# Retention in chunks of 128 tokens with carried states, in place of all keys by all queries, in a two-layer diffusion backbone

## The chip, the cores and the metric

The kernel runs on one core of one Trainium2 chip. The metric is the device time of one execution in microseconds. Three timed runs of the kernel before gave a median of 2387.9 us (2387.57 to 2388.31).

## What is computed

The network has two layers. In each, a modulated norm is followed by one wide input projection, whose columns feed three mixers (a convolution, an attention and a retention), whose outputs are gated, summed and projected; then comes a gated feed-forward part. The latent stream has 512 tokens, the context stream 256; the second layer computes queries for latents only. The change touches the retention. Its reference, for 8 heads of 64 features, runs over chunks of 128 tokens with a state of 64x64 per head, once forward and once backward; the scans of the latents start from the states that the scans of the context end with:

```python
def step(state, inp):
    qc, kc, vc = inp
    inner = jnp.einsum('bihd,bjhd->bhij', qc, kc) * decay_in
    o = (jnp.einsum('bhij,bjhe->bihe', inner, vc)
         + jnp.einsum('bihd,bhde->bihe', qc * q_dec[:, :, None], state))
    state = state * chunk_dec[:, None, None] + jnp.einsum('bjhd,bjhe->bhde', kc * k_dec[:, :, None], vc)
    return state, o

o_cf, s_f = retention_scan(q_c, k_c, v_c, log_gamma[0], s0)
o_cb, s_b = retention_scan(flip(q_c), flip(k_c), flip(v_c), log_gamma[1], s0)
o_lf, _ = retention_scan(q, k, v, log_gamma[0], s_f)
o_lb, _ = retention_scan(flip(q), flip(k), flip(v), log_gamma[1], s_b)
```

## The kernel before

Activations lie feature by token: a tile of 128 features by 768 tokens, latents in columns 0 to 511 and context in 512 to 767. A dense product takes every float32 operand as two float32r parts (`hh` and `hl` for activations, `whi` and `wlo` for weights) and sums three products of parts in PSUM (`chunk`, `dense`, L242 to L254); its tiles in PSUM are called `pd` and have four banks, all other products (`ps`) have the other four. Weights stream through SBUF once; ScalarE and VectorE split each tile of 1024 columns into its parts (`prepare`, L99).

The mixers are generators that run beside the dense products: after every product `tick` gives each of them credit, and each `yield` of a generator spends some (L222, L148). That sets the order in which the program is written; the scheduler of the framework then orders each engine's own list, and an engine works through its list in order. `layer_mixers` (L1273) goes through the units of `ORDER`. A unit P (`ret_inputs`, L1154) makes three dense products for a pair of heads: keys, queries and gate. The retention of the pair, `ret_gen` (L709), is run by `mixers` (L1288) once the attention is done, beside the units P of the next pairs and the gates T; there are four pairs in each layer.

The retention takes all keys by all queries. For each pair of heads, `evac_split` (L578) splits keys and queries into float32r parts, and `stack` (L1145) lays the parts of a head above each other by transfers on GpSimd's queue, so that one product with 128 rows makes two of the three products of parts and one with 64 rows the third. For each of the six key tiles there are two score tiles of 128 keys by 512 queries (and 256 context queries in the first layer), which VectorE multiplies by the decays (tile `rsc`, L750). `decay` (L689) makes the decays of one head for all distances, five exponentials on ScalarE and four operations on VectorE. Then `pv` multiplies the scores by the values in plain float32, 64 output rows for each head side by side, and sums over the key tiles in PSUM.

After that (L763 on, not changed) come the squares, the product with a block matrix (`ro`), the reciprocal root and the gate.

Of the kernel before, what the change touches and what calls it, by code (L numbers as in the profile page):

```python
"""Hybrid conv / GQA / retention DiT backbone on one core.

Activations are feature-major: a [128, T] tile per 128 features, with the latent tokens in
columns 0..511 and the context tokens in columns 512..767. Dense products run on the tensor
engine in float32r: every float32 operand is split exactly into two float32r parts and three
products of parts are accumulated. Weights stream through SBUF once, in the order of use.
"""
# [8 lines left out]
F32 = mybir.dt.float32  # L16
# [6 lines left out]
P = 128  # L23
# [10 lines left out]
SUB = 1024                      # columns of a weight tile  # L34
NSUB = 140                      # weight tiles of a layer
START = ((0, 256, 2), (256, 256, 0), (512, 256, 4), (768, 256, 0))  # columns of the first modulation, weight tiles after
ND = 4                          # PSUM banks of the dense products
RAWB, RAWA = 2, 2               # tiles of raw weights, of raw w_ada
WB = 4                          # split weight tiles
NSLOT = 47                      # activation tiles  # L40
# per layer: order of the units of the input projection (K keys and values, Q queries, R retention values,
# A attention and retention begin, G inputs of the convolution, C it begins, P retention heads, T gates)
ORDER = ('K Q0 R0 Q1 A R1 G0 C G1 G2 G3 P0 P1 P2 P3 T T T T',
         'K Q0 Q1 R0 A G0 C R1 G1 G2 G3 P0 P1 P2 P3 T T T T T T')
ATT_LEAD, RET_LEAD = (3, 2), (1, 1)   # head pairs by which the mixers may lag behind the projection
# [1548 lines left out]
```

## Time and profile before

| what | value |
|---|---|
| timed runs | 2387.9 us median of 3 (2387.57 to 2388.31) |
| span of the profiled execution, first to last instruction | 2385.8 us (its own time is not listed apart) |
| TensorE (PE) busy | 2347.9 us, 98% of the span |
| VectorE (DVE) busy | 1566.2 us, 66% |
| ScalarE (ACT) busy | 896.0 us, 38% |
| chain that ended last | PE 95%, DVE 3%, issue 1%, DMA 1% |
| mean DMA rate | 98 GB/s |

Busy time is the time in which an engine had at least one instruction in work; matmuls overlap at their ends, so the busy times of single groups add up to more than the engine's. What a group costs the engine is read from the distance between starts, or from what is left of a stretch when all else in it is taken off.

### The profile page before, as it was taken

The page shows a single profiled execution, that of the slowest core. Times are in us where ns is not written, and L with a number is a line of the kernel's source. Part 1 is how long each engine was busy: PE and PEld are TensorE (multiplying, and loading weights), DVE is VectorE, ACT ScalarE, POOL GpSimd, SP SyncE. Part 2 cuts the span into 40 slices and gives each one's busy share as a digit, 9 for nine tenths or more (in the row PEclk, how much of TensorE's full clock was granted, in tenths as well). Part 3 has the DMA queues.
Part 4 walks back from the last instruction along what each step waited for, and adds up shares of the span by engine and source line. Part 5 has one row for each costly group of instructions (what it writes and reads, how often), then busy time and mean ns, then how long its engine had stood idle before and what let it go on. Part 6 is the DMA issues. An engine that isn't in the chain of part 4 may idle for free.

```text
span 2385.8 us, 33890 instructions
## 1 busy us (share of the span) xinstructions
PE 2347.9 (98%) x13426; PEld 1941.3 (81%) x13426; DVE 1566.2 (66%) x3174; ACT 896.0 (38%) x1505; POOL 62.6 (3%) x122
## 2 busy tenths in 40 slices
PE   6999999999999999999999999999999999999998
PEld 5988876678888888888888889887558889888887
DVE  6887858688874476645763359878688546544445
ACT  3465644422232342213122234565443433423233
POOL 0000010000000000000000000001100000000000
PEclk9999999999999999999999999999999999999999
DMA  7221122213343123323661121113223322332322
GB/s 287 96 65 60 63 80 69 71 62 115 107 142 105 54 73 118 118 97 101 210 210 62 62 98 54 55 61 102 70 67 112 131 98 80 106 97 97 97 97 71
DMA packets 69119, 234.13 MB, mean 98 GB/s; under 512 B 8640, under 2 KB 10960, under 8 KB 68960
## 3 DMA queue, kind: packets, MB, share of 16 engines
q1 hardware_dynamic: 59616, 203.64, 25.8%
q0 software_dynamic: 9344, 28.32, 4.1%
q8 instruction: 106, 1.74, 0.3%
q14 instruction: 53, 0.43, 0.1%
HBM read 213.57 MB, written 6.82 MB: 92 GB/s over the span
## 4 chain that ended last, share of the span: by engine, by line
PE 95%; DVE 3%; issue 1%; DMA 1%; ACT 0%; SPq 0%; DVEq 0%; ACTq 0%
PE pd L197 81%; PE ps L197 12%; PE ps L1090 2%; DVE ht L543 0%; DVE wlo L108 0%; PE ps L1003 0%; DVE hl L555 0%; DMA x<-xt 0%; DVE qq L1038 0%; DMA raw<-wstream 0%; ACT whi L107 0%; DVE sq L508 0%; DVE mod L418 0%; DVE rstdt L491 0%; DVE rstd L492 0%
## 5 line engine op out<-in xcount | busy, mean ns | idle before, releaser
L197 PE MATMUL pd<-hl,whi 128*128 128x512 f32 (+1 forms) x2176 | 658.6, 354 | 1.9 <-DVE hl L555 1.7
L197 PE MATMUL pd<-hh,wlo 128*128 128x512 f32 (+1 forms) x2176 | 659.9, 355 | 0.0
L197 PE MATMUL pd<-hh,whi 128*128 128x512 f32 (+1 forms) x2176 | 656.9, 354 | 1.4 <-DVE fy L1387 0.9
L107 ACT ACTIVATE whi<-raw 128x1024 fp32r<-128x1024 f32 x280 | 296.7, 1061 | 930.9 <-PE pd L197 840.6
L108 DVE TENSOR_TENSOR wlo<-raw,whi 128x1024 fp32r<-128x1024 f32 x280 | 341.6, 1221 | 261.8 <-ACT whi L107 258.7
L197 PEld LDWEIGHTS pd<-hh,whi 128*128 128x128 f32 x2176 | 361.9, 188 | 69.5 <-issue 8.3
L197 PEld LDWEIGHTS pd<-hl,whi 128*128 128x128 f32 x2176 | 360.3, 188 | 68.9 <-issue 8.3
L197 PEld LDWEIGHTS pd<-hh,wlo 128*128 128x128 f32 x2176 | 360.8, 188 | 64.6 <-issue 9.4
L608 DVE SCALAR_TENSOR_TENSOR cacc<-u,vec,cacc 128x497 f32<-128x497 f32 (+9 forms) x360 | 221.4, 648 | 1.9
L197 PE MATMUL pd<-hidh,wlo 128*128 128x512 f32 (+1 forms) x558 | 169.1, 348 | 0.0
L197 PE MATMUL pd<-hidh,whi 128*128 128x512 f32 (+1 forms) x558 | 167.9, 346 | 0.0
L197 PE MATMUL pd<-hidl,whi 128*128 128x512 f32 (+1 forms) x558 | 167.3, 345 | 0.0
L1073 ACT ACTIVATE prob<-ps,amx,qrs 128x256 f32<-128x256 f32 (+1 forms) x144 | 93.7, 656 | 90.8 <-DVE amx L1068 77.5
L197 PE MATMUL pd<-whi,hl 128*128 128x256 f32 x416 | 120.1, 289 | 3.9 <-DVE hl L555 3.9
L197 PE MATMUL pd<-whi,hh 128*128 128x256 f32 x416 | 120.5, 292 | 2.8 <-ACT hh L552 2.8
L197 PE MATMUL pd<-wlo,hh 128*128 128x256 f32 x416 | 119.3, 287 | 0.0
L1430 DVE SCALAR_TENSOR_TENSOR x<-pd,mod,x 128x512 f32<-128x512 f32 (+1 forms) x102 | 62.1, 632 | 81.0 <-PE pd L197 80.7
L466 DVE SCALAR_TENSOR_TENSOR rowa<-rowa,crow 128x768 f32<-128x768 f32 (+1 forms) x144 | 94.2, 686 | 26.2 <-DMA rowa<-wadt 26.2
L197 PEld LDWEIGHTS pd<-hidh,whi 128*128 128x128 f32 x558 | 94.9, 189 | 14.9 <-issue 0.2
L1395 DVE TENSOR_TENSOR fy<-fy,pd 128x512 f32<-128x512 f32 x66 | 37.5, 596 | 104.2 <-PE pd L197 101.4
L197 PEld LDWEIGHTS pd<-hidl,whi 128*128 128x128 f32 x558 | 93.7, 188 | 14.1 <-issue 0.2
L197 PEld LDWEIGHTS pd<-hidh,wlo 128*128 128x128 f32 x558 | 94.3, 189 | 13.0
(236 smaller groups left out, 3251.4 us busy)
## 6 DMA issues: line engine op xcount, KB each, us to landing
raw<-wstream SPq DMA_DIRECT2D x280, 512.0 KB, 3.5
rowa<-wadt SPq DMA_DIRECT2D x72, 512.0 KB, 4.1
adar<-wada SPq DMA_DIRECT2D x16, 384.0 KB, 7.6
stk<-rkh POOLq DMA_DIRECT2D x32, 192.0 KB, 4.9
rawa<-wada SPq DMA_DIRECT2D x8, 512.0 KB, 3.6
x<-xt SPq DMA_DIRECT2D x8, 384.0 KB, 7.6
x<-xt POOLq DMA_DIRECT2D x8, 384.0 KB, 4.4
adar<-wada SPq DMA_DIRECT2D x8, 256.0 KB, 7.5
```

The costliest lines, as they stand in the source:

```text
L107: nc.scalar.activation(hi, r, AF.Copy)
L108: nc.vector.tensor_tensor(lo, r, hi.bitcast(F32), op=ALU.subtract)
L197: return self.nc.tensor.matmul(out, w, x, start=start, stop=stop)
L466: nc.vector.scalar_tensor_tensor(out, raw[:, a:b], 1.0, t[:, o:o + b - a], op0=ALU.mult, op1=ALU.mult, accum_out=acc[:, c, j, h:h + 1])
L608: nc.vector.scalar_tensor_tensor(acc[:, a:b], u[:, a + d:b + d], w(k), acc[:, a:b], op0=ALU.mult, op1=ALU.add)
L1073: nc.scalar.activation(pr[:, o - k0:o - k0 + c], pt[:, :c], AF.Exp, scale=rs, bias=mx[:, 2:3], accum_out=sm[:, j:j + 1])
L1090: nc.tensor.transpose(pt[:, b * P:b * P + P], pr[:, o + b * P:o + b * P + P], self.ident)
L1395: nc.vector.tensor_tensor(y[:, o:o + n], y[:, o:o + n], pt, op=ALU.mult)
L1430: nc.vector.scalar_tensor_tensor(xs[m][:, s], pt, g2[:, m, j:j + 1], xs[m][:, s], op0=ALU.mult, op1=ALU.add)
```

## The change

It replaces the retention by the chunkwise form of the reference, for the two heads of a pair side by side in the 128 features.

- Keys and queries stay plain float32 (`plain`): no split, no `stack`, no transfers for them.
- TensorE transposes the six key tiles to token-major; VectorE multiplies them by the decays to the end and to the start of a chunk (`kf`, `kb`).
- Scores are made only between tokens of the same chunk: for each chunk and head a float32 product with 64 rows, 128 by 128, the two heads on the two halves of the rows. VectorE multiplies them by a decay of 128x128 that is the same for all chunks.
- Ten products of 128x128 make the contributions of the chunks to the forward and backward states of both heads (the blocks between different heads are masked to zero with `blk`); VectorE scales them and carries the states from chunk to chunk (`stf`, `stb`, L796 after the change).
- The outputs of a pair are summed in PSUM: the scores by the values, 64 rows for each head, and the states by the decayed queries (`qf`, `qb`), with all 128 rows.
- `decay(p)` makes six exponentials of 128 columns for a pair. `ret_tables` makes small tables once in a layer.
- `pe_order` keeps the products of a group in order on TensorE; with arguments, the first product of the group waits for those instructions, so that the group doesn't begin before all of its operands are there.

The diff, cut to the new code (the code that it replaces is printed above; comments are left out):

```diff
 @@ in place of evac_split(), decay(h), stack() and the body of ret_gen()
+    def ret_tables(self):
+        nc = self.nc
+        self.kdec, self.lgx, self.gx = self.sm(16, "kdec"), self.sm(8, "lgx"), self.sm(8, "gx")
+        ij = self.ij
+        for d in range(2):
+            nc.scalar.activation(self.kdec[:, 8 * d:8 * d + 8], self.lg[:, 8 * d:8 * d + 8], AF.Exp,
+                                 scale=ij[:, 4 * P + d:4 * P + d + 1])
+        l4 = self.lg.rearrange("q (c t) -> q c t", t=2)
+        for t in range(2):
+            r = slice(64 * t, 64 * t + 64)
+            nc.vector.tensor_copy(self.lgx[r].rearrange("q (c o) -> q c o", o=1), l4[r, :, t:t + 1])
+        nc.scalar.activation(self.gx, self.lgx, AF.Exp, scale=float(P))
+    def decay(self, p):
+        nc = self.nc
+        w = self.S("dec")
+        ij = self.ij
+        ex = lambda o, i, sc: nc.scalar.activation(w[:, o * P:o * P + P], ij[:, i * P:i * P + P], AF.Exp, scale=sc)
+        for t in range(2):
+            h = 2 * p + t
+            ex(t, 0, self.lg[:, h:h + 1])
+            ex(2 + t, 1, self.lg[:, 8 + h:9 + h])
+        ex(4, 2, self.lgx[:, p:p + 1])
+        ex(5, 3, self.lgx[:, 4 + p:5 + p])
+        f, b = (w[:, o:o + 2 * P].rearrange("p (t i) -> p t i", t=2) for o in (0, 2 * P))
+        for x, m in ((f, self.mf), (b, self.mb)):
+            nc.vector.tensor_tensor(x, x, m.rearrange("p (o i) -> p o i", o=1).to_broadcast([P, 2, P]), op=ALU.mult)
+        nc.vector.tensor_tensor(w[:, 0:2 * P], w[:, 0:2 * P], w[:, 2 * P:4 * P], op=ALU.add)
+        return w
+    @contextmanager
+    def pe_order(self, *after):
+        traced = self.nc.cur_bb.bb.instructions
+        n = len(traced)
+        yield
+        info = lambda c: mybir.DependencyInfo(c, mybir.DependencyReason.DATA)
+        last = None
+        for i in traced[n:]:
+            if i.engine != mybir.EngineType.PE:
+                continue
+            if last:
+                self.tc.add_manual_dep(i, last, info(mybir.DependencyClass.NoSync), reason="order")
+            else:
+                for a in after:
+                    self.tc.add_manual_dep(i, a.ins.name, info(mybir.DependencyClass.Sync), reason="together")
+            last = i.name
+    def ret_gen(self, p, rk, rq, sg, ctxq):
+        nc = self.nc
+        nq = 6 if ctxq else 4
+        w = self.decay(p)
+        yield 2.5
+        bc = lambda t, n: t.rearrange("p (o i) -> p o i", o=1).to_broadcast([P, n, P])
+        v3 = lambda t, n: t.rearrange("p (c i) -> p c i", c=n)
+        tile = lambda t: slice(t * P, t * P + P)
+        heads = lambda hh: slice(64 * (2 * p + hh), 64 * (2 * p + hh) + 64)
+        kt = [self.ps(), self.ps()]
+        with self.pe_order():
+            for t in range(6):
+                nc.tensor.transpose(kt[t // 4][:, tile(t % 4)], rk[:, tile(t)], self.ident)
+        kf, kb = self.S("kf"), self.S("kb")
+        def keys(d, dst, o, src, a, n):
+            dec = self.kdec[:, 8 * d + 2 * p:8 * d + 2 * p + 2].rearrange("p (o h e) -> p o h e", o=1, e=1)
+            return nc.vector.tensor_tensor(
+                dst[:, o * P:(o + n) * P].rearrange("p (c h d) -> p c h d", c=n, h=2),
+                src[:, a * P:(a + n) * P].rearrange("p (c h d) -> p c h d", c=n, h=2),
+                dec.to_broadcast([P, n, 2, 64]), op=ALU.mult)
+        keys(0, kf, 0, kt[1], 0, 2)
+        keys(1, kb, 0, kt[1], 0, 2)
+        keys(0, kf, 2, kt[0], 0, 3)
+        last_k = keys(1, kb, 2, kt[0], 1, 3)
+        yield 1.0
+        scs = [self.S("rsc") for _ in range(2)]
+        lasts = []
+        for a, n in ((0, 4), (4, 2))[:1 + ctxq]:
+            pts = [self.ps() for _ in range(2)]
+            with self.pe_order():
+                for t in range(n):
+                    for hh, pt in enumerate(pts):
+                        r = slice(64 * hh, 64 * hh + 64)
+                        self.mm(pt[:, tile(t)], rk[r, tile(a + t)], rq[r, tile(a + t)], t == 0, t == n - 1)
+            for hh, (sc, pt) in enumerate(zip(scs, pts)):
+                lasts.append(nc.vector.scalar_tensor_tensor(
+                    v3(sc[:, a * P:(a + n) * P], n), v3(pt[:, :n * P], n), 0.125, bc(w[:, tile(hh)], n),
+                    op0=ALU.mult, op1=ALU.mult))
+            yield 0.25 * n
+        F, B = self.S("stf"), self.S("stb")
+        order = ([(kf, 0, 4), (kf, 1, 5), (kf, 2, 0), (kf, 3, 1)],
+                 [(kb, 1, 5), (kb, 0, 4), (kb, 4, 3), (kb, 3, 2)],
+                 [(kf, 4, 2), (kb, 2, 1)])
+        sts = []
+        with self.pe_order(last_k):
+            for part in order:
+                st = self.ps()
+                sts.append(st)
+                for j, (k, i, t) in enumerate(part):
+                    self.mm(st[:, tile(j)], k[:, tile(i)], self.rv[t][:, 2 * p * 64:2 * p * 64 + P], j == 0,
+                            j == len(part) - 1)
+        scale = lambda o, i, n: nc.vector.scalar_tensor_tensor(
+            v3(o, n), v3(i, n), 8.0, bc(self.blk, n), op0=ALU.mult, op1=ALU.mult)
+        scale(F[:, :4 * P], sts[0], 4)
+        scale(B[:, :4 * P], sts[1], 4)
+        scale(F[:, 4 * P:5 * P], sts[2][:, :P], 1)
+        scale(B[:, 4 * P:5 * P], sts[2][:, P:2 * P], 1)
+        for j in range(1, 5):
+            for d, x in enumerate((F, B)):
+                nc.vector.scalar_tensor_tensor(x[:, tile(j)], x[:, tile(j - 1)], self.gx[:, 4 * d + p:4 * d + p + 1],
+                                               x[:, tile(j)], op0=ALU.mult, op1=ALU.add)
+        qf, qb = self.S("qf"), self.S("qb")
+        for x, n, o in ((qf, nq, 4), (qb, nq - ctxq, 5)):
+            lasts.append(nc.vector.tensor_tensor(v3(x[:, :n * P], n), v3(rq[:, :n * P], n), bc(w[:, tile(o)], n),
+                                                 op=ALU.mult))
+        yield 2.6
+        yield 1.0
+        po = self.ps()
+        pc = self.ps() if ctxq else None
+        with self.pe_order(*lasts):
+            for t in range(nq):
+                out, j = (po, t) if t < 4 else (pc, t - 4)
+                for hh, sc in enumerate(scs):
+                    self.mm(out[64 * hh:64 * hh + 64, tile(j)], self.rv[t][:, heads(hh)], sc[:, tile(t)], j == 0, False)
+            for t in range(4):
+                self.mm(po[:, tile(t)], F[:, tile(1 + t)], qf[:, tile(t)], False, False)
+                self.mm(po[:, tile(t)], B[:, tile(4 - t)], qb[:, tile(t)], False, t == 3)
+            if ctxq:
+                self.mm(pc[:, tile(1)], F[:, tile(0)], qf[:, tile(5)], False, False)
+                self.mm(pc[:, tile(0)], B[:, tile(0)], qb[:, tile(4)], False, True)
+        yield 2.9 + 0.8 * ctxq
+        segs = ALL if ctxq else LAT
...
+    def plain(self, pts, m, name):
+        t = self.S(name)
+        for pt, o, c in pts:
+            self.nc.scalar.activation(t[:, o:o + c], pt, AF.Identity, bias=self.bias_col(m))
+        return t
+    def ret_inputs(self, p, segs, T):
+        rk = self.plain(self.win(18 + p, ALL), 18 + p, "rk")
+        self.tick(self.cost)
+        rq = self.plain(self.win(14 + p, segs), 14 + p, "rq")
+        self.tick(self.cost)
+        pg = self.win(26 + p, segs)
...
 @@ in mixers()
-            self.ii, self.jj = self.S("ii"), self.S("jj")
-            nc.gpsimd.dma_start(self.ii, io["ij"][0])
-            nc.gpsimd.dma_start(self.jj, io["ij"][1])
+            self.ij = self.S("ij")
+            nc.gpsimd.dma_start(self.ij[:, :4 * P + 2], io["ij"])
+            self.ret_tables()
...
 @@ in _shape_constants()
-    ij = np.stack([np.maximum(t[None] - p[:, None], 0), np.maximum(640 + p[:, None] - t[None], 0)]).astype(np.float32)
+    i, j = p[None] + 0 * p[:, None], p[:, None] + 0 * p[None]
+    ij = np.concatenate([np.maximum(i - j, 0), np.maximum(j - i, 0), i + 1, P - i, P - 1 - p[:, None], p[:, None]],
+                        1).astype(np.float32)
```

On TensorE, for the first pair of heads of the first layer, before: `stk` are stacked parts of keys and queries, `rqh` and `rkl` the parts of the third product, `rsc` the decayed scores, `rv` the values.

```order
L197 MATMUL ps_4049<-rsc_4063,rv_826 64x512
L197 MATMUL ps_4049<-rsc_4064,rv_826 64x512
L197 MATMUL ps_4089<-stk_3647,stk_3454 128x512
L197 MATMUL ps_4090<-stk_3650,stk_3457 128x512
L197 MATMUL ps_4089<-rqh_3641,rkl_3449 128x512
L197 MATMUL ps_4090<-rqh_3641,rkl_3449 128x512
L197 MATMUL ps_4049<-rsc_4075,rv_826 64x512
L197 MATMUL ps_4049<-rsc_4076,rv_826 64x512
```

Two key tiles stand here; a pair has six of them, with scores of 512 queries each, and dense products lie between some of them.

On TensorE, for the second pair of the first layer, now, behind the transposes, four pairs of latent scores and thirteen dense products among them: `rq`, `rk` are queries and keys of both heads, `kf`, `kb` the decayed keys.

```order
L197 MATMUL pd_4435<-hh_410,whi_4123 128x512
L197 MATMUL ps_4367<-rq_4177,rk_4011 128x128
L197 MATMUL ps_4366<-rq_4177,rk_4011 128x128
L197 MATMUL ps_4367<-rq_4177,rk_4011 128x128
L197 MATMUL ps_4376<-rv_827,kf_4346 128x128 x2
L197 MATMUL ps_4376<-rv_826,kf_4346 128x128 x2
L197 MATMUL ps_4381<-rv_827,kb_4347 128x128 x3
L197 MATMUL ps_4381<-rv_826,kb_4347 128x128
L197 MATMUL ps_4386<-rv_826,kf_4346 128x128
L197 MATMUL ps_4386<-rv_826,kb_4347 128x128
```

The context scores and the states' contributions follow each other; then 27 dense products stand before the scores by the values.

On VectorE, for the first pair of the first layer, before: `deca`, `decb` are the decays of a head, `cacc` the convolution.

```order
L750 SCALAR_TENSOR_TENSOR rsc_4087<-ps_4089,deca_3957 128x512
L750 SCALAR_TENSOR_TENSOR rsc_4088<-ps_4090,deca_4037 128x512
L750 SCALAR_TENSOR_TENSOR rsc_4099<-ps_4101,decb_3958 128x512
L750 SCALAR_TENSOR_TENSOR rsc_4100<-ps_4102,decb_4038 128x512
L750 SCALAR_TENSOR_TENSOR rsc_4099<-ps_4109,deca_3957 128x256
L750 SCALAR_TENSOR_TENSOR rsc_4100<-ps_4110,deca_4037 128x256
L599 TENSOR_SCALAR cacc_4120<-u_2589,vec_86 128x768
L608 SCALAR_TENSOR_TENSOR cacc_4120<-u_2589,vec_86,cacc_4120 128x497
```

And now, for the second pair: `kdec`, `dec`, `gx` are decays, `kf` and `kb` the keys (the last of four), `stf` and `stb` the states.

```order
L752 TENSOR_TENSOR kb_4347<-ps_4338,kdec_3937 128x384
L771 SCALAR_TENSOR_TENSOR rsc_4352<-ps_4354,dec_4328 128x512
L771 SCALAR_TENSOR_TENSOR rsc_4353<-ps_4355,dec_4328 128x512
L771 SCALAR_TENSOR_TENSOR rsc_4352<-ps_4366,dec_4328 128x256
L771 SCALAR_TENSOR_TENSOR rsc_4353<-ps_4367,dec_4328 128x256
L788 SCALAR_TENSOR_TENSOR stf_4374<-ps_4376,cst 128x512
L788 SCALAR_TENSOR_TENSOR stb_4375<-ps_4381,cst 128x512
L788 SCALAR_TENSOR_TENSOR stf_4374<-ps_4386,cst 128x128
L788 SCALAR_TENSOR_TENSOR stb_4375<-ps_4386,cst 128x128
L796 SCALAR_TENSOR_TENSOR stf_4374<-stf_4374,gx_3939 128x128
L796 SCALAR_TENSOR_TENSOR stb_4375<-stb_4375,gx_3939 128x128
```

The last two operations stand three times more, then `qf` and `qb` (768 and 640 columns) close the chain; in this pair no operation of the convolution stands inside it, and 26 to 31 of them stand between one chain and the next.

## Rows read from the trace of the kernel before

**Rows 1.** the profile's page, parts 1 and 4: busy time; the chain that ended last
```profile
PE 2347.9 (98%) x13426; PEld 1941.3 (81%) x13426; DVE 1566.2 (66%) x3174; ACT 896.0 (38%) x1505; POOL 62.6 (3%) x122
...
PE 95%; DVE 3%; issue 1%; DMA 1%; ACT 0%; SPq 0%; DVEq 0%; ACTq 0%
```

**Rows 2.** two stretches, PE: length, busy (instructions), granted clock, DMA share, GB/s
```profile
330.00:512.00 182.00, 182.00 (x846) 1.00 0.24 66
1653.50:1792.00 138.50, 138.50 (x552) 1.00 0.28 74
```

**Rows 3.** PE's groups by form from 330 to 512: busy, mean ns, idle before
```profile
L197 PE MATMUL pd<-hh,whi 128*128 128x512 f32 x95 | 38.6, 406 | 0.0
...
L197 PE MATMUL ps<-rsc,rv 128*64 128x512 f32 x96 | 36.2, 615 | 0.0
...
L197 PE MATMUL pd<-hh,whi 128*128 128x256 f32 x96 | 27.3, 284 | 0.0
```

**Rows 4.** PE's groups by form from 1653.5 to 1792
```profile
L197 PE MATMUL pd<-hl,whi 128*128 128x512 f32 x100 | 41.3, 413 | 0.0
...
L197 PE MATMUL pd<-hh,whi 128*128 128x256 f32 x17 | 4.9, 291 | 0.0
```

**Rows 5.** timeline of PE, dense products alone: start us, us, form, count
```profile
899.71 0.53 PE L197 MATMUL pd<-hh,wlo 128*128 128x512 f32 x2
...
904.66 0.51 PE L197 MATMUL pd<-hl,whi 128*128 128x512 f32 x2
...
1659.18 0.39 PE L197 MATMUL pd<-hh,whi 128*128 128x512 f32 x1
...
1664.39 0.39 PE L197 MATMUL pd<-hh,wlo 128*128 128x512 f32 x1
```

**Rows 6.** timeline of PE, one key tile without dense products
```profile
345.08 0.73 PE L197 MATMUL ps<-stk,stk 128*128 128x512 f32 x2
345.74 0.50 PE L197 MATMUL ps<-rqh,rkl 64*128 64x512 f32 x2
346.17 1.08 PE L197 MATMUL ps<-rsc,rv 128*64 128x512 f32 x4
347.18 0.73 PE L197 MATMUL ps<-stk,stk 128*128 128x512 f32 x2
```

**Rows 7.** timeline of PE, transposes and plain float32 products of 128 to 512 columns
```profile
201.29 0.60 PE L1090 MATMUL ps<-cst,prob 128*128 128x128 f32 x4
...
203.72 0.38 PE L1090 MATMUL ps<-cst,prob 128*128 128x128 f32 x2
...
204.39 1.53 PE L197 MATMUL ps<-probt,vt 128*64 128x128 f32 x24
205.85 0.50 PE L197 MATMUL ps<-kh,qq 128*128 128x512 f32 x1
...
362.19 1.56 PE L197 MATMUL ps<-ro,cst 128*128 128x512 f32 x4
363.39 0.47 PE L197 MATMUL pd<-hh,wlo 128*128 128x256 f32 x1
```

**Rows 8.** timeline of DVE, operations back to back
```profile
386.12 0.29 DVE L704 TENSOR_TENSOR dect<-dect,cst 128x128 f32<-128x128 f32 x1
386.32 0.82 DVE L706 TENSOR_TENSOR decb<-decb,dect 128x640 f32<-128x640 f32 x1
387.06 0.29 DVE L705 TENSOR_TENSOR deca<-deca,dect 128x128 f32<-128x128 f32 x1
```

**Rows 9.** instructions on the tile ro: duration ns min/median/max
```profile
L197 PE MATMUL ps<-ro,cst x24: 378/592/697, 362.2 to 1791.0; 128*128 128x512 f32 x16, 128*128 128x256 f32 x8
```

**Rows 10.** DVE from 330 to 695: length, busy; its waits from 330 to 700
```profile
330.00:695.00 365.00, 289.87 (x537) 1.00 0.29 88
...
DVE rsc L750 <- PE ps L197: 32.0, 26, 4.7
```

**Rows 11.** ACT's groups: table loads, busy, mean ns
```profile
L563 ACT ACT_TABLE_LOAD x11 | 14.1, 1283 | 0.2
```

More of the change, by code (lines that the diff above doesn't have):

```diff
@@ L709, in ret_gen @@
     def ret_gen(self, p, rk, rq, sg, ctxq):
         nc = self.nc
-        (kd, kl), (qd, qh) = rk, rq
-        ws = []
-        for hh in range(2):
-            ws.append(self.decay(2 * p + hh))
-            yield 3.0
+        nq = 6 if ctxq else 4
[5 more added lines that the diff above has]
+        heads = lambda hh: slice(64 * (2 * p + hh), 64 * (2 * p + hh) + 64)
@@ L729, in ret_gen @@
-        for kt in range(6):
-            kk = slice(kt * P, kt * P + P)
-            kc = kt if kt < 4 else kt - 4
-            scs = [self.S("rsc") for _ in range(2)]
-            for o, c in ALL if (ctxq and kt >= 4) else LAT:
-                pts = [self.ps()[:, :c] for _ in range(2)]
-                for pt, k, q in zip(pts, kd, qd):
-                    self.mm(pt, k[:, kk], q[:, o:o + c], True, False)
-                for hh, pt in enumerate(pts):
-                    rr = slice(64 * hh, 64 * hh + 64)
-                    self.mm(pt, kl[rr, kk], qh[rr, o:o + c], False, True)
-                for sc, pt, (wa, wb) in zip(scs, pts, ws):
-                    if o:
-                        parts = [(0, CTX, wa, 384 - 128 * kc)]
-                    elif kt == 0:
-                        parts = [(0, 384, wa, 384), (384, SEQ, wb, 640)]
-                    elif kt < 4:
-                        parts = [(0, SEQ, wa, 384 - 128 * kc)]
-                    else:
-                        parts = [(0, SEQ, wb, 128 - 128 * kc)]
-                    for a, b, w, d in parts:
-                        nc.vector.scalar_tensor_tensor(sc[:, o + a:o + b], pt[:, a:b], 0.125, w[:, d:d + b - a],
-                                                       op0=ALU.mult, op1=ALU.mult)
-                yield 0.0014 * c
-            if pend:
-                pv(*pend)
-            pend = kt, scs
-            yield 0.9
@@ L1142, in glu @@
         return u
-    def stack(self, a, b, w):
-        out = []
-        for hh in range(2):
-            t = self.S("stk", F32R)
-            for i, x in enumerate((a, b)):
-                self.nc.gpsimd.dma_start(t[64 * i:64 * i + 64, :w], x[64 * hh:64 * hh + 64, :w])
-            out.append(t)
-        return out
+    def plain(self, pts, m, name):
[3 more added lines that the diff above has]
+        return t
     def ret_inputs(self, p, segs, T):
-        nc = self.nc
-        kh, kl = self.evac_split(self.win(18 + p, ALL), 18 + p, "rk")
-        rk = self.stack(kh, kh, TALL), kl
+        rk = self.plain(self.win(18 + p, ALL), 18 + p, "rk")
         self.tick(self.cost)
-        qh, ql = self.evac_split(self.win(14 + p, segs), 14 + p, "rq")
-        rq = self.stack(qh, ql, T), qh
+        rq = self.plain(self.win(14 + p, segs), 14 + p, "rq")
         self.tick(self.cost)
@@ L1306, in mixers @@
                 self.ret_done += 1
-            self.rvt = self.rv = self.ii = self.jj = None
+            self.rvt = self.rv = self.ij = None
         us = [None] * 4
```

37 lines of the change are left out of this document (1 added, 36 removed).

## The prediction

> **What bounds the kernel now.** I read the page first: TensorE is busy for 98% of the span, and 95% of the chain that ended last lies on it [rows 1]. So a change is worth what it takes from TensorE's list, less what it adds in waits. Next I cut out the two stretches in which the retention runs: 182.0 us in the first layer, 138.5 us in the second, TensorE busy throughout, the granted clock at 1.00 [rows 2]. The groups by form say what else lies in them. In the first: 95 or 96 of each of the three kinds of dense products at 512 columns and as many at 256, so 288 of each width [rows 3]. In the second: some 301 at 512 and 51 at 256 [rows 4]. Busy times of groups overlap, so I price a product by the distance between starts: 14 steps of a 512 and a 256 together from 899.71 to 904.66 are 0.3536 us each, and 23 single 512s from 1659.18 to 1664.39 are 0.2265 us each [rows 5]; a 256 is the difference, 0.127.
>
> **What is removed.** First layer: 182.0 - 288 x 0.3536 (101.8) - four sums of `ro` at 1.20 each (362.19 to 363.39 [rows 7]; 4.8) leaves 75.4 us for scores and values of four pairs. Second layer: 138.5 - 301 x 0.2265 (68.2) - 51 x 0.127 (6.5) - four `ro` of 512 columns (two thirds of 1.20; 3.2) leaves 60.6. Together 136.0 us. A check: a key tile without dense products takes 2.10 us (345.08 to 347.18 [rows 6]), so six of them take 12.6 and, with the context's queries on two more, some 15 to 16 for a pair; four pairs would be 62, and the interleaving, which splits the pairs of heads that run together, makes the rest. These 136.0 us stand on the path, since TensorE never pauses there.
>
> **What is added on TensorE**, for a pair of heads.
> - Six transposes. Four take 0.60 and two 0.38 from first start to last end [rows 7], so one more is 0.11: 0.66 us.
> - Values: 12 products of 64 output columns by 128, in float32, two heads together. Attention has just that group: 24 records from 204.39 to 205.85, 1.46 us with entry and exit [rows 7]. Second layer, four chunks: 0.97.
> - States and carried states, full float32 products of 128x128. There is no such row. Lower bound: 1.20 us for the 768 columns of `ro`, so 0.20 for 128. A product leaves two records, and two passes at the pace of a transpose give 0.22; I take that. Ten for the states 2.20; for the outputs ten (2.20), eight in the second layer (1.76).
> - Scores, 64 rows by 128. No row shows it in plain float32. The nearest is the pair of split products with 64 rows, whose two heads run together: two of 512 columns in 0.43 [rows 6]. So I price a pair of heads like the values' (1.46 for six chunks, 0.97 for four). The upper bound is one head after the other, 0.22 each and 0.20 for entry and exit (0.43 less 0.2265), which adds 1.4 a pair in the first layer and 1.0 in the second, 9.6 us in all. In the last three pairs of the first layer the order cuts the scores into three pieces: 0.40 more each.
>
> First layer: 4 x 7.98 + 1.2 = 33.1. Second: 4 x 6.56 = 26.2. Sum 59.3, so TensorE's list is 76.7 us shorter.
>
> **The waits that are added.** Three places: context scores need the PSUM banks of the transposes, so they wait for VectorE's four key products; the states wait for the decayed scores to free theirs; the outputs wait for VectorE's whole chain. VectorE's price comes from operations back to back: 0.20 us at 128 columns, 0.74 at 640 [rows 8], so 0.34 at 256, 0.47 at 384, 0.60 at 512, 0.87 at 768. The chain of a pair in the first layer: keys 1.6, decays 1.0, scores 1.9, states 1.6, eight recurrences 1.6, `qf` and `qb` 1.6; 9.3 us. From the end of the transposes to the outputs TensorE's order holds 1.9 us of scores, 2.2 of states and 3 + 10 + 27 dense products at 0.177 (7.1): 11.1 us. So the chain is covered with 1.8 us to spare in the second pair; if the convolution's operations stood in front of it, the spare would be gone. In the first pair no dense product stands between scores and states: some 0.7 us of wait for the keys, 0.3 for the banks and 0.5 for the squares ahead of `ro`. The second layer has shorter chains and 10 to 23 dense products at each place. I take 1 us for each of the eight pairs, 8 us; the bounds are 0 and 25, the latter if every pair waits for a third of its chain.
>
> **The other edits.** VectorE loses work: a pair of the first layer cost 8.7 (scores) + 2.7 (decays of two heads) + 1.9 (low parts), 13.3 us, against 9.3. ScalarE loses exponentials and gets two table loads of 1.28 us [rows 11] in front of two weight tiles early in the first layer: nothing, as the split tiles are four deep; 2.6 us if that cover fails. On GpSimd's queue 64 transfers of `stack` and two of the four tables go; nobody waits behind the one that stays but the first decays, as before. On SyncE's queue one weight load passes one row of the modulation, with others already in flight: nothing.
>
> **The sum.** Span 2385.8 - 76.7 + 8 = 2317.1. The timed runs lie 2.1 us above the span (2387.9), which is what stands around it: **2319 us**. With the bounds above (3 us less where 152 products take 0.20, no waits; 9.6 us more for scores one after the other, some more waits) this case gives 2308 to 2334.
>
> **Rival 1: VectorE sets the pace in the first layer.** From one pair's keys to the next its list holds 26 to 31 operations of the convolution (about 14 us), the chain of 9.3, the root and gate and three weight tiles: some 34 us, and TensorE's list is about 35. From 330 to 695 VectorE was busy for 289.9 of 365 us [rows 10]; its work falls by 16 us, TensorE's by 38 after waits. If all of its 75 idle us stayed, it would need 349 us where TensorE needs 327: 22 us late, 2341. Against it: 32.0 us of that idle time were waits for TensorE's scores [rows 10], which go.
>
> **Rival 2: the weight loads come into the open.** The new products are 128 columns wide, so each pass has a load of its own behind a short product. A first pass that has to wait for its load lasts 697 ns where the second lasts 592 [rows 9], 0.105 us more. With 304 passes of full float32 products and 48 transposes that makes 37 us: 2356. Against it: the four transposes, each with another stationary tile, follow each other at 0.11 us [rows 7], and 128 columns at two cycles of 2.4 GHz are 0.107. The Trainium skill, "TensorE: Matmul & The Clock Gate", section "The mechanism", speaks for this rival: a load overlaps products in flight only where their row groups differ, which would lay all 352 loads open. By that rule the time would be the 2356 of this rival; the transposes, which share all rows, disagree at 0.11 us each.
>
> **Rival 3, slower: TensorE waits for VectorE in every pair.** TensorE takes its list in order, so whatever is late there stops the dense products behind it too. If the chain had no cover (9.3 less 3.7 of TensorE's own work of the pair, 5.6 us, eight times) and VectorE came to it with the convolution's 14.3 us still ahead in the first layer (four times), the waits would be 102 us: 2413. It decides from 9.6 us of wait a pair, where the gain is used up. Against it: the order shows 27 dense products there, and no convolution inside the chain.
>
> **How the numbers follow.** A difference of 0.2%, 4.8 us, is about what a measurement can tell from none. Forecast 0.72; rival 1 0.13; rival 2 0.06; rival 3 0.03; below 2308 0.04, where VectorE's relief shortens stretches that I left alone; 0.02 for a gain that comes back wholly as a wait further on. Range 2308 to 2348: the forecast's own range and rival 1 with some margin, 0.85. Faster is the forecast with rivals 1 and 2 and the case below 2308, 0.95; same 0.02; slower rival 3, 0.03.
>
> **What would show it.** Right: some 60 us for the new products in the two stretches, full products at 0.22, scores of two heads starting together, TensorE still at 98% or close. The stretch from the first scores to the last `ro` shorter by about 38 us in the first layer and 30 in the second. Wrong: waits of TensorE for `kf`, `rsc` or `qb` above 2 us a pair (rivals 1, 3), products of 128 columns at 0.4 us (rival 2), scores at 0.44 a chunk, or a new idle time of TensorE where the convolution's branch begins.

## The result and the profile after

The changed kernel takes 2320.1 us (median; 2319.3 to 2324.3) where the kernel before took 2388.0 in runs on the same chip: a ratio of 0.9719, 95% interval 0.9707 to 0.9731. Its profiled execution has a span of 2318.8 us. The forecast was 2319.

The page of the kernel after, parts 1 and 4 (busy time; the chain that ended last):

```profile
PE 2278.0 (98%) x13650; PEld 1953.7 (84%) x13650; DVE 1536.5 (66%) x3150; ACT 866.7 (37%) x1481; POOL 28.4 (1%) x56
...
PE 92%; DVE 5%; ACT 1%; issue 1%; DMA 0%; SPq 0%; DVEq 0%; ACTq 0%
```

TensorE is busy for the same 98%, with 69.9 us less in it [rows 1], and idle for 2.9 us more; so the 67 us of the span came from its list. To see where, both kernels are cut at the first retention product and the start of the last record of `ro` in each layer (columns: stretch, length, busy, instructions, granted clock, DMA share, GB/s). The kernel before:

```profile
330.61:500.44 169.83, 169.83 (x777) 1.00 0.24 64
1654.21:1790.96 136.75, 136.75 (x545) 1.00 0.28 75
```

The kernel after:

```profile
331.85:464.52 132.67, 131.26 (x896) 1.00 0.14 47
1617.49:1715.53 98.04, 97.34 (x610) 1.00 0.16 54
```

The first layer's stretch is 37.2 us shorter. The second's is 38.7 shorter, but 38 dense products of 512 columns have left it; at 0.2265 us each they are 8.6, and 30.1 is the retention's. That is 67.3 us. Of the rest of the program, the part ahead of the first stretch is 1.2 us longer, the part between the two 0.8 shorter, and the part behind the second 8.4 longer, about what the 38 products take. TensorE is now idle for 1.4 and 0.7 us. Its groups by form in the first layer's retention (busy, mean ns, idle before) say for what:

```profile
L197 PE MATMUL ps<-rq,rk 64*128 64x128 f32 x96 | 9.2, 292 | 1.4 <-DVE kb L752 1.3
L197 PE MATMUL ps<-qf,stf 128*128 128x128 f32 x40 | 8.1, 285 | 0.0
...
L197 PE MATMUL ps<-rv,kf 128*128 128x128 f32 x40 | 6.2, 285 | 0.0
L197 PE MATMUL ps<-rsc,rv 128*64 128x128 f32 x96 | 6.1, 277 | 0.0
...
L747 PE MATMUL ps<-cst,rk 128*128 128x128 f32 x24 | 3.3, 272 | 0.0
```

One wait is left in this layer, for the scaled keys (`kb`) ahead of the context's scores; in the second layer the states wait for `kb` (0.7 us). The outputs (`qf`, and `rsc`) wait for nothing. The first pair's products follow each other like this (timeline of PE: start us, us, form, count):

```profile
331.85 0.82 PE L747 MATMUL ps<-cst,rk 128*128 128x128 f32 x6
332.59 2.34 PE L197 MATMUL ps<-rq,rk 64*128 64x128 f32 x24
334.86 1.16 PE L197 MATMUL ps<-rv,kf 128*128 128x128 f32 x8
...
337.11 0.59 PE L197 MATMUL pd<-hh,whi 128*128 128x512 f32 x2
...
343.07 1.53 PE L197 MATMUL ps<-rsc,rv 128*64 128x128 f32 x24
344.53 0.49 PE L197 MATMUL ps<-qf,stf 128*128 128x128 f32 x2
344.85 0.39 PE L197 MATMUL ps<-qb,stb 128*128 128x128 f32 x2
...
346.78 0.36 PE L197 MATMUL pd<-hl,whi 128*128 128x256 f32 x1
```

From start to start, that is from a group's first start to the next group's: transposes 0.74, scores 2.27 (a wait within), states 2.25, values (the scores by the values) 1.46, carried outputs (the states by the decayed queries) 2.25. Added up from start to start over all eight pairs, transposes are 6.0, scores 13.0, states 17.8, values 9.9, carried outputs 16.3: 63.0 us where the sum had 59.3. Added up in the same way, the scores of the kernel before take 68.2 us and its values 61.9, 130.1 together. So the new products in place of the old ones are 67.1 us, the whole gain. The dense products of the two stretches, with the waits that follow them, took 169.9 us before and take 161.1 now, the moved 38 apart the same.

### The profile page after: what moved, and what is told of

The parts are those of the page before. It is cut to its first block, busy times and chain, and to the rows that moved or that the text cites. A ratio compares the mean times of both kernels' runs of the same rounds, so it can differ in the third digit from the quotient of the medians.

```text
span 2318.8 us, 34073 instructions
## 1 busy us (share of the span) xinstructions
PE 2278.0 (98%) x13650; PEld 1953.7 (84%) x13650; DVE 1536.5 (66%) x3150; ACT 866.7 (37%) x1481; POOL 28.4 (1%) x56
## 4 chain that ended last, share of the span: by engine, by line
PE 92%; DVE 5%; ACT 1%; issue 1%; DMA 0%; SPq 0%; DVEq 0%; ACTq 0%
PE pd L197 81%; PE ps L197 9%; PE ps L1149 2%; DVE wlo L108 1%; DVE cacc L598 1%; DVE ht L543 0%; PE ps L1062 0%; ACT whi L107 0%; DVE hl L555 0%; DMA x<-xt 0%; DVE qq L1097 0%; DVE sq L508 0%; DVE kb L752 0%; DVE mod L418 0%; DVE kf L752 0%
```

## The experiments

**The arithmetic of the scores without the chunks.** The kernel before, with keys and queries left whole:

```diff
-                for pt, k, q in zip(pts, kd, qd):
-                    self.mm(pt, k[:, kk], q[:, o:o + c], True, False)
                 for hh, pt in enumerate(pts):
                     rr = slice(64 * hh, 64 * hh + 64)
-                    self.mm(pt, kl[rr, kk], qh[rr, o:o + c], False, True)
+                    self.mm(pt, rk[rr, kk], rq[rr, o:o + c], True, True)
```

> The kernel before with one part of the change alone: its scores become plain float32 products of two heads side by side, still all keys by all queries; no states, no split and stacked keys and queries. Theory (the gain comes from the chunks, that is from fewer columns; the form of the scores is worth next to nothing): a key tile's scores took 1.09 us in the split form (0.66 and 0.43) and take two passes of 512 columns for a pair of heads, 0.9 us and 0.2 for entry and exit, so 1.1 us; time 2380 to 2392, the same as before within 0.3%. Rival (the split and stacked form, with its 64 transfers and its work for VectorE, was what cost): more than half of the 68 us comes already, 2355 or less. A third way: dense products get between the two heads of a key tile and break the pairs, 0.45 us each on up to 56 pairs, up to 2410.

Measured: 2388.9 us, ratio to before 1.0002 (0.9993 to 1.0012). One key tile in its timeline of PE, from 336.60 to 338.67, is 2.07 us where it was 2.10 [rows 6]:

```profile
336.60 1.13 PE L197 MATMUL ps<-rq,rk 64*128 64x512 f32 x4
337.66 1.08 PE L197 MATMUL ps<-rsc,rv 128*64 128x512 f32 x4
```

The new form alone brings no time. But it is not shown to cost TensorE what the old one did. The page of this run, part 1, and TensorE's waits in the first layer (326 to 500) and the second (1640 to 1800):

```profile
PE 2336.5 (98%) x13426; PEld 1928.7 (81%) x13426; DVE 1552.3 (65%) x3146; ACT 895.4 (38%) x1505; POOL 29.6 (1%) x58
```

```profile
PE ps L197 <- DVE rsc L747: 6.8, 12, 1.1
```

```profile
PE ps L197 <- DVE rsc L747: 2.9, 4, 1.1
```

TensorE is busy for 11.4 us less than before [rows 1] (the scores alone take 59.4 us start to start without the waits, where they took 68.2), and it waits 9.7 us for VectorE's decayed scores, where the kernel before has no wait. So the theory's time held, and its reason only in part: the form shortened the list, and new waits took that back. What `stack` and the low parts cost GpSimd and VectorE cannot be read from this run alone; the next one tells form and columns apart.

**The chunks with the old arithmetic.** The changed kernel, with scores of split and stacked keys and queries:

```diff
-                    for hh, pt in enumerate(pts):
-                        r = slice(64 * hh, 64 * hh + 64)
-                        self.mm(pt[:, tile(t)], rk[r, tile(a + t)], rq[r, tile(a + t)], t == 0, t == n - 1)
+                    for pt, k, q in zip(pts, kd, qd):
+                        self.mm(pt[:, tile(t)], k[:, tile(a + t)], q[:, tile(a + t)], t == 0, False)
+                for t in range(n):
+                    for hh, pt in enumerate(pts):
+                        r = slice(64 * hh, 64 * hh + 64)
+                        self.mm(pt[:, tile(t)], kl[r, tile(a + t)], qh[r, tile(a + t)], False, t == n - 1)
```

> The changed kernel with the chunks' scores in the split form of the kernel before (keys and queries in two parts, stacked by transfers: two full products for a pair of heads and two of 64 rows with the low parts), each of 128 columns; chunks, states and the rest as in the change. Theory (the split form costs three passes of 0.11 us for a pair of heads and a chunk where the plain one costs two, and VectorE gets two low parts of 0.87 us a pair of heads): 40 chunks by 0.11 are 4.4 us, one more entry of 0.2 per group 2 to 3 us, 2326 (2322 to 2334). Rival (products of split parts are slow at 128 columns, so that the plain form is a large part of the change): 0.22 or more a pass, 2338 or more.

Measured: 2329.7 us, ratio 0.9758 (0.9741 to 0.9774), within the range of the first theory. So the chunks, that is the fewer columns, give 59 of the 68 us with the old form, and the plain form with what goes with it is worth some 10 us more. Its timeline of PE, four chunks of a pair:

```profile
331.65 1.09 PE L197 MATMUL ps<-stk,stk 128*128 128x128 f32 x8
332.67 0.66 PE L197 MATMUL ps<-rqh,rkl 64*128 64x128 f32 x8
333.26 0.50 PE L197 MATMUL pd<-hh,whi 128*128 128x512 f32 x1
```

They take 1.61 us, against 1.09 in the changed kernel (368.31 to 369.40). Start to start, all scores take 16.5 us against 13.0; TensorE's waits in the two stretches are 8.5 us against 2.0 and make the rest.

**One head's scores after the other's.**

```diff
-                for t in range(n):
-                    for hh, pt in enumerate(pts):
+                for hh, pt in enumerate(pts):
+                    for t in range(n):
```

> The changed kernel with the scores of a pair's first head all issued before those of the second, instead of alternating chunk by chunk; all else as it is. Theory (the two heads use two halves of the array's rows and run at the same time only if they are neighbours in the order): each of the 40 chunks costs 0.22 us more, 8.8 us in all, 2329 (2326 to 2332). Rival (the heads follow each other anyway, and starts 7 ns apart are only how the records are written): no change, 2320 within 2.

Measured: 2321.4 us, ratio 0.9724 (0.9709 to 0.9738), which cannot be told from the change. My theory's number missed, and the time is the rival's. But the trace does not bear the rival out. Start to start, the scores take 17.5 us, 4.5 more, not 8.8. In the second layer the 16 records of a pair show it; first the changed kernel, then this one (timeline of PE):

```profile
1618.23 1.16 PE L197 MATMUL ps<-rq,rk 64*128 64x128 f32 x16
```

```profile
1617.55 1.71 PE L197 MATMUL ps<-rq,rk 64*128 64x128 f32 x16
1619.18 0.50 PE L197 MATMUL pd<-hh,whi 128*128 128x512 f32 x1
```

0.55 us more for four chunks, where 0.88 was expected: the second head's products begin while the first's still run. Alternating, the eight products of these records take 1.09 us, where one after the other at 0.224 they would take 1.79. So the overlap of the two heads is real, but it does not need them to alternate strictly. (The Trainium skill, "TensorEngine Tiling (Array Packing)", section "Key Properties", says that different tiles of the array can work in parallel; the trace agrees, with 17.5 us where one after the other would be 21.8.) Of the 4.5 us, 2.0 fell into the waits for `kb`, which are gone from this trace: the keys are ready by the time the longer scores end. Where the rest went is open; the medians differ by 1.3 us, less than their intervals can tell.

**No fixed order within groups.** The loop of `pe_order` runs over nothing, so neither the order within a group nor the common start is set, and the planner (the framework's scheduler) orders TensorE's list alone.

> The changed kernel with the fixed order inside the four groups of products of a pair, and the two groups' common start, taken out: the planner then puts 12 value products straight behind the states, and cuts the carried outputs into 2 and 8 with dense products between them. Theory (TensorE waits little either way, grouping saves only some switches between full and half array of 0.2 us): 1 to 3 switches more a pair, and up to 1.5 us of wait for the decayed scores a pair, 2322 to 2332. Rival (grouping is what keeps TensorE from waiting): 5 us a pair or more, 2360. Rival (the grouping costs more than it gives): under 2317.

Measured: 2321.8 us, ratio 0.9722 (0.9708 to 0.9737): 0.2 us below the range of the first theory, and not to be told from the change. The planner's own order is as good here.

**More work in VectorE's chain.** `qf` and `qb` are made four times over, and in a second kernel nine times:

```diff
-            lasts.append(nc.vector.tensor_tensor(v3(x[:, :n * P], n), ...
+            for _ in range(4):
+                op = nc.vector.tensor_tensor(v3(x[:, :n * P], n), ...
+            lasts.append(op)
```

> The changed kernel with six more multiplications for VectorE in the chain of every pair (each of the two that make qf and qb is done four times): 4.8 us a pair in the first layer, 3.6 in the second, 34 us in all. The planner puts 55 to 61 dense products in front of the outputs where 27 to 33 stood. Theory (VectorE has some 7 idle us a pair in the first layer's retention and the chain can be covered with more dense products): 0 to 5 us more, 2320 to 2325. Rival 1 (VectorE sets the pace of the first layer): the 19 us of the first layer all show, 2339 or more. Rival 3 (TensorE waits out the chain in every pair): all 34 us show, 2354.

> The same with sixteen more: 12.9 us a pair in the first layer, 9.6 in the second, 90 us in all. Theory: the first layer's 51.6 us stand against 56 us that VectorE is idle between 330 and 660 us, 28 of them in the retention itself, so that some 24 us cannot be held in that stretch and only part of it is made good later; the second layer (19 idle us from 1600 to 1720, 38 added) loses some 20 as well: 2335 to 2370. Rival 1 (VectorE sets the pace already): 2372 (first layer) and more. A theory by which VectorE never matters: 2320.

Measured: 2322.5 us with 34 us added (ratio 0.9728, 0.9714 to 0.9741), and 2376.4 us with 90 added (0.9954, 0.9941 to 0.9968). The smaller dose costs 2 us, too little to be told from nothing: rival 1 would have shown 19. VectorE's busy time from 325 to 475, in the changed kernel and with the smaller dose:

```profile
325.00:475.00 150.00, 121.89 (x237) 1.00 0.15 52
```

```profile
325.00:475.00 150.00, 136.67 (x254) 1.00 0.15 49
```

The idle time takes the work up, and the planner moves the first layer's outputs behind 55 to 61 dense products (34 to 37 in the second). The larger dose does not fit. It costs 56 us, 6 above the upper end that I gave, and its number alone would fit rival 1 too (2372 and more); it is the smaller dose that speaks against that rival. TensorE now waits in both layers. Its waits from 325 to 505, and the windows where the granted clock is lowest:

```profile
PE ps L197 <- DVE qb L801: 12.9, 3, 9.6
PE ps L197 <- DVE ry L843: 4.0, 2, 2.0
PE ps L747 <- DVE rrstdt L490: 2.9, 2, 2.1
```

```profile
450.00:475.00 25.00, 21.98 (x130) 0.86 0.14 43
475.00:500.00 25.00, 15.38 (x93) 0.80 0.24 74
```

What I had left out: around these waits the granted clock is below 1.00, so TensorE also runs slower. The next experiment shows that at a single wait.

**No cover for the chain.** The two `yield`s ahead of a pair's outputs are gone, and in `mm` the next 80 products are ordered behind the pair's last one (`hold`), so that dense products come behind the pair and not into it:

```diff
+        if self.hold and self.hold[1]:
+            self.hold[1] -= 1
+            self.tc.add_manual_dep(i.ins, self.hold[0], info, reason="order")
```

> The changed kernel with all dense products kept out of a pair: scores, states, values and carried outputs of a pair stand one behind the other in TensorE's list, and the dense products that lay between them (27 to 33 before the outputs, 13 among the scores) follow the pair. Nothing else differs. Theory (the cover is what keeps VectorE's chain off the path): TensorE waits from the end of the states for qb, 5 to 5.5 us a pair in the first layer and 4 to 4.5 in the second, some 40 us, less 2 to 4 us for waits and switches that go: 2357 (2345 to 2370). Rival 3 in full (VectorE also comes to the chain with the convolution's operations ahead of it): 2400 or more. Rival (the chain is so short that cover is not needed): under 2330.

Measured: 2396.5 us, ratio 1.0041 (1.0027 to 1.0055): slower than the kernel before. Its waits, first layer (325 to 510), then second (1640 to 1785):

```profile
PE ps L198 <- DVE qb L806: 18.8, 4, 5.4
PE ps L198 <- DVE kb L758: 7.5, 6, 1.4
```

```profile
PE ps L198 <- DVE qb L806: 16.0, 4, 4.1
PE ps L198 <- DVE kb L758: 12.3, 4, 3.2
```

For `qb` TensorE waits 34.8 us, near the 38 of the theory (5.25 and 4.25 us, four times each). My number was 40 us too low because of two things. The waits for `kb` ahead of the context's scores or the states, 19.8 us, were not in it: the dense products among the scores had covered these too. And products after a wait are slow. Timeline of PE and the windows around the first wait:

```profile
343.04 2.83 PE L198 MATMUL ps<-rsc,rv 128*64 128x128 f32 x24 [5.36 <-DVE qb L806]
345.80 0.69 PE L198 MATMUL ps<-qf,stf 128*128 128x128 f32 x2
```

```profile
337.00:343.00 6.00, 0.67 (x7) 0.99 0.30 87
343.00:346.00 3.00, 2.96 (x25) 0.50 0.00 0
346.00:350.00 4.00, 4.00 (x26) 0.97 0.00 0
```

After 5.36 us without a product, the values' group runs at a granted clock of 0.50, the level of 1.2 GHz, and takes 2.83 us where it took 1.53. Over all pairs the values take 18.6 us instead of 9.9, start to start, and the carried outputs 23.5 instead of 16.3. Of the 76.4 us lost against the change, 52.6 are waits (54.6 less the change's 2.0); some 24 are left. The slower values and carried outputs make 15.9 of them; the rest was not taken apart.

**The states twice.** Each group of state products is issued a second time into the same banks (`list(enumerate(part)) * 2`).

> The changed kernel with each group of ten state products of a pair issued twice over (the second pass writes the same states again). Theory (a full float32 product of 128 columns is two passes of 0.112 us with its weight loads hidden, and whatever stands in TensorE's list counts in full): 80 products by 0.224 us are 17.9 us, less up to 2 us of waits that they cover, 2337 (2335 to 2339). Rival 2 (weight loads lie open): 0.43 a product, 34 us, 2354. Rival (TensorE's list has slack that the products can fall into): under 2330.

Measured: 2341.3 us, ratio 0.9807 (0.9794 to 0.982), 21.2 us above the change and 2 above the range of the theory; rival 2 would have shown 34. Start to start, the states take 35.8 us instead of 17.8: 17.9 more, just 0.224 us a product, with a weight load for each of its passes. One pair, from 334.12 to 338.61:

```profile
334.12 2.05 PE L197 MATMUL ps<-rv,kf 128*128 128x128 f32 x16
336.01 1.95 PE L197 MATMUL ps<-rv,kb 128*128 128x128 f32 x16
...
338.61 0.48 PE L197 MATMUL pd<-hh,whi 128*128 128x512 f32 x1
```

The two stretches, with their dense products taken off, are 18.5 longer. The other 3 us are not explained; they are no more than the two intervals leave open (some 3 us each way for either ratio).

**Column halves.** A version meant to be faster. A state product of 128x128 also computes the two blocks between different heads, which are then masked to zero; here each head has a product of its own, of 64 by 64, on one half of the array's columns:

```diff
-                    self.mm(st[:, tile(j)], k[:, tile(i)], self.rv[t][:, 2 * p * 64:2 * p * 64 + P], ...
+                    for hh in range(2):
+                        self.mm(st[half(hh), slot(j)], k[:, i * P + 64 * hh:i * P + 64 * hh + 64],
+                                self.rv[t][:, heads(hh)], ...
...
-                self.mm(po[:, tile(t)], F[:, tile(1 + t)], qf[:, tile(t)], False, False)
+                    for hh in range(2):
+                        r = half(hh)
+                        self.mm(po[r, tile(t)], x[r, slot(j)], q[r, tile(t)], ...
```

> A version meant to be faster: the state products of the two heads are not 128x128 with the off-diagonal blocks thrown away, but one of 64 output rows by 64 columns for each head, side by side in the two halves of the array's columns, and the outputs from states are 64x64 products of the two heads side by side; the states are half as wide, so VectorE's eight recurrences and four scalings too, and nothing is masked. Theory (a pass costs its columns, so a pair of heads' state product costs two passes of 64 columns, 0.056 each): 10 products by 0.11 us less, 8 pairs, 9 us, less one more switch of 0.2 a pair or two: 2313 (2310 to 2316). Rival (a pass costs at least its weight load, 0.11): nothing is gained and a switch is paid, 2320 to 2323.

Measured: 2313.4 us, ratio 0.969 (0.9677 to 0.9704), as the theory had it. The states of a pair take 1.41 us (333.59 to 335.00) instead of 2.25:

```profile
333.59 0.69 PE L197 MATMUL ps<-rv,kf 128*64 128x64 f32 x16
334.15 0.69 PE L197 MATMUL ps<-rv,kb 128*64 128x64 f32 x16
...
335.00 0.62 PE L197 MATMUL pd<-hh,whi 128*128 128x512 f32 x2
```

**Both directions in one product**, on top of that. A head's forward state lies on 64 rows and its backward state on the other 64, with the queries copied to both (`twice`), so one product gives both carried outputs:

```diff
+        rq = rq, self.twice(rq, T)
...
+            for t in range(nq):
+                out, j = (po, t) if t < 4 else (pc, t - 4)
+                for h in range(2):
+                    self.mm(out[64 * h:64 * h + 64, tile(j)], xv[:, h, t, :], qs[h][:, tile(t)], False, t in (3, 5))
```

> A further step on the version with column halves: for each head the forward state lies on 64 rows and the backward state on the other 64, and the scaled queries likewise (a copy of the queries for the other 64 rows by four transfers a pair), so that one product of 128 rows and 64 columns for a head and a chunk gives both directions, in the same form as the values' products. TensorE's carried outputs become 6 pairs of heads' products instead of 10 (4 instead of 8 in the second layer); VectorE gets 8 recurrence operations more a pair (some 1.5 us) in the chain. Theory (VectorE's longer chain is covered by more dense products): 4 products by 0.22 us and a switch of 0.15 to 0.2 less a pair, 1.05 us by 8, 8.4 us below the version with column halves (2313): 2305 (2303 to 2309). Rival (the longer chain or the transfers on GpSimd's queue come onto the path): 2313 or more.

Measured: 2313.1 us, ratio 0.969 (0.9677 to 0.9703): no gain, as the rival had it. TensorE's list did get shorter: the outputs take 9.8 us start to start instead of 16.9. But the longer chain now ends too late. TensorE's waits for the scaled queries (`qs`), 4.5 us, first and second layer:

```profile
PE ps L197 <- DVE qs L810: 1.8, 4, 0.5
```

```profile
PE ps L197 <- DVE qs L810: 2.7, 4, 0.8
```

The order also cuts the states of all four pairs of the first layer in two pieces with dense products between them (in the first pair they start at 333.75 and 334.68), which costs an entry each, a longer step to the first product of another form; how much that makes was not measured. The scaling of the queries does not need the states, so in a last version it is written ahead of them:

> The version with stacked directions, with the two scalings of the queries written ahead of the states (they do not depend on them), so that VectorE's chain ends with the recurrences; the planner then sets 37 to 41 dense products ahead of the outputs where it set 35. Theory (what the stacked version lost against its 2305 is mostly the 4.5 us for which TensorE waited for the scaled queries in eight pairs, the rest switches where the states are cut in two pieces): 3 to 4 us of the waits go, 2309 (2307 to 2312). Rival (the loss lies elsewhere): 2313 as before.

Measured: 2309.9 us, ratio 0.9672 (0.9659 to 0.9685). The waits at that place (now for the states, `stx`) are 0.3 and 2.2 us, 2.0 less in all, where 3 to 4 were expected. The median is 3.2 us lower, but the intervals of the two versions overlap, so what this step gave is not shown. By the median it is the fastest version of this study, 10.2 us below the change.

## Why the prediction was right

- **What is removed, 136.0 us.** Too high, by about 6. The way of reckoning repeats: the stretches before are 169.8 and 136.8, and without the dense products in them (252 of each width, and 295 with 48) and the eight `ro`, they leave 137.3. But scores and values took 130.1 of that, start to start. The other 7 us lay in the dense products among them, which took 0.240 us at 512 columns in the first stretch and 0.243 in the second, not the 0.2265 of a row of their own kind. After the change they take 0.240 and 0.245, some of it waits, so most of these 7 us stayed.
- **What is added, 59.3 us.** Measured start to start, 63.0, 6% above. The values' price from attention's group held to the hundredth (1.46). A full float32 product of 128 columns took 0.224 where 0.22 was taken. The scores were mis-sized: 13.0 us where (4 x 1.46 + 4 x 0.97 + 1.2) gives 10.9; a whole group of four chunks takes 1.09 where 0.97 was put down, and the pieces in which the first layer's order cuts them cost more than their 0.40 (some of it is wait).
- **The waits, 8 us.** Too high: 2.1 us of idle time in the two stretches. The named cause was right in one place, the context's scores behind `kb`; the outputs wait for nothing. VectorE's chain is a little longer than its price: the eight recurrences of the first pair take 2.1 us where 1.6 was put down.
- **The sum.** The two stretches are shorter by 37.2 and 30.1 us, where 38 and 30 were named as a sign of being right. The mechanism held: the list of TensorE got shorter by the old products less the new ones, and the cover kept the chain off the path. That the time came out only about 1 us off is luck in part: the removal was put 6 us too large and the new products 4 us too small, and the waits, put 6 us too high, made up for much of it.
- **The other edits, nothing.** Shown only as a whole: ahead of the first stretch the program is 1.2 us longer, between the two 0.8 shorter. Leaving the split and the stacked copies out of the kernel before changed its time by 0.0002 of it, but there a shorter list and new waits offset each other, so it does not price these edits one by one.
- **Rival 1** did not happen. VectorE is busy for 299.1 us from 330 to 695 (289.9 before [rows 10]; over the whole program it has 29.7 us less), and its waits for scores are gone from its list; 19 us more in the first layer and 14 in the second cost 2. But its margin is finite: with 52 and 38 us more TensorE waits for it.
- **Rival 2** did not happen. Each pass has a load of its own and they follow each other at 0.112 us, also when 80 products are added. By one sentence of the Trainium skill, "TensorE: Matmul & The Clock Gate", section "The mechanism", a load overlaps products in flight only where the row groups differ, so loads of passes that share all rows would lie open (another sentence there excepts loads into a background buffer for weights, which no run here shows). The trace disagrees with the first: 0.112 us against 0.217 if the 0.105 of [rows 9] stood in front of each.
- **Rival 3** is what the change is without its cover. I put it at 102 us of waits and the point at which it decides at 9.6 us a pair. With the cover taken away the loss is 76.4 us, 9.55 a pair, which is more than the gain (1.0041 of the time before); 54.6 of it are waits. Its mechanism was right and its size too large: `qb` is waited for 5.4 us at most, near the 5.6 of a chain without cover and far from what 14 us of the convolution ahead of it would give, while the slower clock, which I had left out, made up part of it.

## What to carry to other kernels

Price products by the distance between starts in a row of the same shape, and count the columns: fewer columns were worth 59 of 68 us here, while the arithmetic form alone shortened the list by 11 us and brought no time, since new waits took it back. A change that shortens the busiest engine's list by adding a chain on another engine is worth what its list loses only while other work of the busy engine stands between the chain's start and its end; check that cover first, since without it the same change was a loss. When a shorter list brings less time than that, look for the new wait, and for work in the chain that can be done before it begins.

## What was not expected

- A wait can cost more than its length: after 5.36 us of idle time TensorE's granted clock was 0.50 for the next 3 us, and 24 records took 2.83 us instead of 1.53. In the changed kernel it is 1.00 throughout both stretches.
- Products on the two halves of the rows overlap even if the first half's eight records all stand ahead of the second's: 1.71 us for 16, where 1.16 is full overlap and 2.04 (1.16 and 0.88) none.
- A pass over 64 columns is about half as long as one over 128, with its own weight load: in the stacked version, passes of a pair of halves start 0.055 us apart, against 0.112.

```profile
333.86 0.22 PE L197 MATMUL ps<-rv,kf 128*64 128x64 f32 x1
...
333.91 0.22 PE L197 MATMUL ps<-rv,kf 128*64 128x64 f32 x1
...
333.97 0.22 PE L197 MATMUL ps<-rv,kf 128*64 128x64 f32 x1
```
